# Sums of a Strassen-form down projection moved into gate-and-up, and its seven products taken one after the other over all pairs

## The chip, the core and the metric

The kernel runs on one core of one Trainium2 chip. The metric is the device time of one execution in microseconds (us); each figure is the median of several runs. The engines are TensorE (PE, with its weight loads as PEld), VectorE (DVE), ScalarE (ACT), GpSimd (POOL) and SyncE (SP), which here issues nearly all the DMAs.

## What is computed

One block on x of 1024 tokens x 1024 features in float32. The change touches the two FFNs; between them lies a mixer (an input projection, two kinds of mixing along the tokens, an output projection), which stays as it is.

```python
def swiglu(x, w_gate, w_up, w_down):
    return (jax.nn.silu(x @ w_gate) * (x @ w_up)) @ w_down

x = x + 0.5 * swiglu(rmsnorm(x, ffn1_norm), ffn1_w_gate, ffn1_w_up, ffn1_w_down)
h = rmsnorm(x, mix_norm)
...
x = x + concat([y_a, y_b]) @ w_out
x = x + 0.5 * swiglu(rmsnorm(x, ffn2_norm), ffn2_w_gate, ffn2_w_up, ffn2_w_down)
y = rmsnorm(x, final_norm)
```

w_gate and w_up are 1024 x 2816, w_down is 2816 x 1024.

## The kernel before

**Precision.** Every product keeps float32 accuracy by three matmuls (mm3): each operand is split into a high part (an ACT cast, L61) and a low part (a DVE subtraction, L62), and high x high, high x low and low x high are summed in PSUM.

**Seven products.** Large products are cut 2 x 2 and computed with seven products of sums instead of eight products of blocks. The sums have to be formed beside TensorE.

**Gate-and-up** (`ffn`, loop over c). The 2816 FFN columns are 22 chunks of 128. For each chunk, SP loads two half MB of weights (graw, L186), GpSimd forms four sums (L192), ACT and DVE split them, and PE runs 84 matmuls. Even chunks use four PSUM banks called mm, odd chunks four called ax. DVE and ACT finish the activations sg = silu(gate) * up, which go to DRAM as hd (L280). Chunk 0 is done plainly, by `gu_plain`. The tiles of x that the FFN adds to are loaded after chunk 2 (FFN2 keeps four of the eight in SBUF).

**Down stage.** It multiplies hd (2816 x 1024 tokens) with w_down. Two chunks make a pair, so there are 11 pairs. Pairs 0 to 9 are taken in three groups, of 1 + 1, 2 + 2 and 2 + 2 pairs, and the seven products combine the two pair sets of a group. `group` loads four tiles hx of activations and weights (L300, L301), forms the sums in place on GpSimd (L323; DVE takes some in the first group), splits each product's operands into a tile called unit (three buffers; a unit is two chunks of 128 here), and runs 24 matmuls for each unit. A product's result in its four banks is then added by DVE into the x tiles (L347) or an accumulator acc (L351), or copied by ACT into acc (L354). The plan of a group takes the banks in the order mm, mm, ax, mm, mm, ax, ax: where `start` is true, a new result begins in the banks, which the product before must have left. Units are prepared two ahead of the matmuls. Pair 10 is done plainly at the end, tile of tokens by tile of tokens; after each tile, `emit` hands the finished x tile on: in FFN1 it is stored to xd and normed, and transposed for the mixer (`to_mid`, L520, L95); in FFN2 it is normed and stored to the output (`fin`).

A stage is 936 matmuls of 128 x 128 by 512. The program is written in order and the instructions of each engine are queued in an order that a scheduler makes from it; a queue runs strictly in its order. Of the tiles' pools, gsp has 7 buffers, post 4, cmb 3 and the pool of x tiles 8.

## Time and profile before

| what | value |
|---|---|
| median of 3 runs | 1911.67 us (1911.02 to 1916.76) |
| the profiled execution | 1916.1 us, of which the span is 1914.0 us |
| mean granted TensorE clock | 0.981 |
| GpSimd busy | 665.9 us, 35% |
| DMA traffic | 199.98 MB, mean 104 GB/s |

The page that the profile gives holds the busy time of each engine over the span, slices of it, DMA queues, the chain of work that ended last, and the costliest groups of instructions. Tables by windows and timelines come from the same trace. In a timeline a row reads: start in us, length, engine, line of the kernel, operation, output<-input by the program's names, shape, count, and in brackets the engine's idle time before it and what released it. An engine's share is a mean over stages with different limits, so a stage is read by its own window.

### The profile page before, as it was taken

What the parts mean: (1) busy time and instruction counts of PE and PEld (TensorE: products, weight loads), DVE (VectorE), ACT (ScalarE), POOL (GpSimd) and SP (SyncE); (2) the same over time, 40 slices, a digit from 0 to 9 for tenths busy, and PEclk for the clock granted to TensorE, in tenths of its full rate; (3) what the DMA queues carried; (4) which work ended last, traced back from release to release, by engine and by line L of the source; (5) the groups of instructions that cost most, each with busy time, mean ns of one, the idle gap of its engine ahead of it and who ended that gap; (6) DMA issues with size and microseconds to landing.
All of it is one profiled execution on the core that took longest, in us unless ns stands there. A gap on an engine that the chain in (4) does not pass through costs nothing.

```text
span 1914.0 us, 25049 instructions
## 1 busy us (share of the span) xinstructions
PE 1812.0 (95%) x9759; PEld 1542.0 (81%) x9759; DVE 1253.3 (65%) x1663; ACT 674.2 (35%) x1171; POOL 665.9 (35%) x477
## 2 busy tenths in 40 slices
PE   6999999999798899898999999999999999979888
PEld 5888888887687689797788989988888888768766
DVE  7655555557988984668755236655555555798896
ACT  6333232334233343432354434433333332323233
POOL 4322222224647802221132402242323222454681
PEclk9999999999899999999999999999999999999999
DMA  6222222225222224354432343323232323531312
GB/s 227 92 91 78 88 78 89 77 89 200 89 79 97 84 107 141 122 182 122 130 90 65 118 145 122 115 74 97 68 99 67 99 67 98 171 115 57 119 44 88
DMA packets 95815, 199.98 MB, mean 104 GB/s; under 512 B 23857, under 2 KB 39505, under 8 KB 95697
## 3 DMA queue, kind: packets, MB, share of 16 engines
q1 hardware_dynamic: 93200, 193.95, 30.7%
q10 hardware_dynamic: 2496, 4.44, 0.8%
q8 instruction: 76, 1.25, 0.3%
q14 instruction: 43, 0.34, 0.1%
HBM read 149.06 MB, written 49.30 MB: 104 GB/s over the span
## 4 chain that ended last, share of the span: by engine, by line
PE 71%; DVE 15%; POOL 4%; issue 4%; ACT 3%; DMA 2%; DVEq 0%; POOLq 0%; SPq 0%; ACTq 0%
PE mm L53 40%; PE ax L53 29%; DVE unit L62 6%; DVE x L347 1%; POOL hx L323 1%; DVE acc L852 1%; POOL s L192 1%; PE sd L53 1%; DMA graw<-in_f1gu_dram 1%; PE ax L95 1%; PE sc L53 1%; POOL rs L70 0%; POOL E L778 0%; DVE xn L82 0%; ACT actT L102 0%
## 5 line engine op out<-in xcount | busy, mean ns | idle before, releaser
L53 PE MATMUL mm<-unit 128*128 128x512 f32 x960 | 240.9, 412 | 49.7 <-DVE acc L351 25.8
L62 DVE TENSOR_TENSOR unit<-hx,unit 128x1024 fp32r<-128x1024 f32 x128 | 247.2, 1971 | 45.0 <-ACT unit L61 44.3
L192 POOL TENSOR_TENSOR s<-graw 128x512 f32<-128x512 f32 x84 | 108.5, 1292 | 466.7 <-DMA graw<-in_f1gu_dram 178.9
L53 PEld LDWEIGHTS mm<-unit 128*128 128x128 f32 x960 | 192.0, 201 | 96.6 <-issue 48.9
L62 DVE TENSOR_TENSOR gs<-s,gs 128x512 fp32r<-128x512 f32 x168 | 162.0, 966 | 142.5 <-ACT gs L61 141.7
L61 ACT CAST unit<-hx 128x1024 fp32r<-128x1024 f32 x128 | 128.5, 1050 | 260.9 <-PE mm L53 84.7
L53 PE MATMUL ax<-unit 128*128 128x512 f32 x912 | 211.0, 390 | 4.0 <-DVE unit L62 3.4
L61 ACT CAST gs<-s 128x512 fp32r<-128x512 f32 x168 | 100.2, 620 | 317.9 <-POOL s L192 213.7
L53 PEld LDWEIGHTS ax<-unit 128*128 128x128 f32 x912 | 170.6, 188 | 40.6 <-DVE unit L62 4.2
L53 PE MATMUL ax<-T,gs 128*128 128x512 f32 x792 | 183.1, 389 | 0.0
L53 PEld LDWEIGHTS ax<-T,gs 128*128 128x128 f32 x792 | 148.7, 188 | 30.8
L62 DVE TENSOR_TENSOR ga<-graw,ga 128x512 fp32r<-128x512 f32 x134 | 96.2, 719 | 114.0 <-ACT ga L61 113.7
L53 PE MATMUL mm<-B,ga 128*128 128x512 f32 (+1 forms) x864 | 166.3, 347 | 0.2 <-ACT B L118 0.2
L53 PE MATMUL mm<-T,gs 128*128 128x512 f32 x720 | 166.4, 389 | 0.0
L53 PEld LDWEIGHTS mm<-T,gs 128*128 128x128 f32 x720 | 135.2, 188 | 28.0
L53 PEld LDWEIGHTS mm<-B,ga 128*128 128x128 f32 x864 | 139.7, 194 | 19.5 <-ACT B L118 0.5
L53 PE MATMUL mm<-actT,wk 128*128 128x512 f32 x576 | 152.3, 407 | 1.8 <-ACT ev L713 1.8
L53 PE MATMUL mm<-wk,actT 128*128 128x256 f32 (+1 forms) x1152 | 147.9, 286 | 0.0
L53 PEld LDWEIGHTS mm<-wk,actT 128*128 128x128 f32 x1152 | 141.2, 191 | 0.4
L53 PE MATMUL ax<-B,ga 128*128 128x512 f32 x528 | 126.9, 389 | 0.0
L323 POOL TENSOR_TENSOR hx<-hx 128x1024 f32<-128x1024 f32 x40 | 126.8, 3201 | 0.0
L53 PEld LDWEIGHTS mm<-actT,wk 128*128 128x128 f32 x576 | 105.0, 191 | 21.4 <-ACT ev L713 2.0
(240 smaller groups left out, 2756.4 us busy)
## 6 DMA issues: line engine op xcount, KB each, us to landing
graw<-in_f1gu_dram SPq DMA_DIRECT2D x44, 512.0 KB, 4.3
graw<-in_f2gu_dram SPq DMA_DIRECT2D x44, 512.0 KB, 3.9
hd<-sg SPq DMA_DIRECT2D x42, 512.0 KB, 5.1
hx<-hd SPq DMA_DIRECT2D x40, 512.0 KB, 6.3
hx<-in_f1wd_dram SPq DMA_DIRECT2D x20, 512.0 KB, 6.8
hx<-in_f2wd_dram SPq DMA_DIRECT2D x20, 512.0 KB, 7.4
x<-in_x_dram SPq DMA_DIRECT2D x16, 512.0 KB, 6.1
graw<-in_wo_dram SPq DMA_DIRECT2D x16, 512.0 KB, 3.8
```

The costliest lines, as they stand in the source:

```text
L53: nc.tensor.matmul(*args, **kw)
L61: nc.scalar.copy(h, src)
L62: nc.vector.tensor_tensor(l, src, h, op=ALU.subtract)
L95: nc.tensor.transpose(ps[:, i * P:(i + 1) * P], blk(i), ident)
L192: nc.gpsimd.tensor_tensor(f, u, v, op=op)
L323: eng.tensor_tensor(o, u, v, op=op)
L347: nc.vector.scalar_tensor_tensor(xv, p, 0.5, xv, op0=ALU.mult, op1=ALU.add)
L852: nc.vector.scalar_tensor_tensor(acc, pad[:, j:j + 512], cw[:, blk, j:j + 1], acc, op0=ALU.mult, op1=ALU.add)
```

## The change

The seven products are now formed inside each pair: chunk 2q is one half of the inner dimension and chunk 2q + 1 the other. The sums that this takes are formed in gate-and-up. After an odd chunk's weights are prepared, `weight_sums` loads the pair's rows of w_down (wd), forms four sums on GpSimd and stores them to DRAM as wq; after the odd chunk's products, `hidden_sums` forms four sums of activations on GpSimd and stores seven operands as hq, in place of hd. These tiles live in the pool of x tiles, so the x tiles are loaded after gate-and-up (`load_xts`); FFN2 stores its four kept tiles to xd and loads all eight again.

The down stage runs each of the seven products over all 11 pairs before it goes to the next, in six units of two pairs (the last of one): 7 x 11 x 12 = 924 matmuls. Each unit loads its two operands (left from hq, right from wq or w_down) and splits them. The banks alternate. There is no plain pair at the end: x tiles 0 to 3 are finished after the sixth product, and 4 to 7 in the last units of the seventh.

```diff
--- before.py
+++ after.py
@@ -170,11 +170,18 @@
         for _ in islice(zip_longest(*parts), n):
             pass
-    def ffn(cb, wgu, wd, ps, gp, qp, bp, start, emit, before={}):
+    def ffn(cb, wgu, wd, ps, gp, qp, bp, start, load_xts, emit, before={}):
         A, X = (ps[0], "mm"), (ps[1], "ax")
         gu_s = {}
         B = cb.B
-        hd = [dr.tile([2, P, T], F32, tag=f"hd{i}", name=f"hd{i}") for i in range(NCH // 2)]
+        hq = [dr.tile([P, 7, 2, 512], F32, tag=f"hq{i}", name=f"hq{i}") for i in range(6)]
+        wq = [dr.tile([P, 4, 2, 512], F32, tag=f"wq{i}", name=f"wq{i}") for i in range(6)]
+        hid = {}
+        def whole(name):
+            return xp.tile([P, 2, 512], F32, tag="x", name=name)
         def gtile(dt, name):
             return gp.tile([P, 2, 512], dt, tag="gsp", name=name, bufs=7)
@@ -237,28 +244,25 @@
                 first = x[1] == "1"
                 for p, wt in ((gates[i], g["B11" if first else "a12"]), (ups[i], g["a21" if first else "a22"])):
                     products(p, wt, xs[x], sl, first, not first)
-            sg = gp.tile([P, 2, w], F32, tag="sf", name="sg", bufs=3)
+            if 0 not in hid:
+                hid[0] = whole("sg")
+            sg = hid[0][:, :, sl]
             for i in range(2):
                 nc.scalar.activation(sg[:, i], gates[i], AF.Silu)
                 nc.vector.tensor_tensor(sg[:, i], sg[:, i], ups[i], op=ALU.mult)
-            nc.sync.dma_start(hd[0][0].rearrange("p (b n) -> p b n", b=2)[:, :, sl], sg)
-        def gu(c, pp, sl=slice(0, 512)):
+        def post(n):
+            return qp.tile([P, 2, 512], F32, tag="post", name=n, bufs=4)
+        def gu(c, pp):
             g = gu_s[c]
-            w = sl.stop - sl.start
-            pa, pb, pc, pd = (bank(*pp)[:, :w] for _ in range(4))
+            pa, pb, pc, pd = (bank(*pp) for _ in range(4))
             def prod(p, n, first, last):
-                products(p, g[n], lambda s, k, sl: B[n][:, s, k, sl], sl, first, last)
-            def post(n):
-                return qp.tile([P, 2, 512], F32, tag="post", name=n, bufs=4)
-            if w == 512:
-                pe, up, sg = post("pe"), post("up"), post("sg")
-            else:
-                both, sg = post("pe"), post("sg")
-                pe, up, sg = both[:, :, :w], both[:, :, w:], sg[:, :, :w]
+                products(p, g[n], lambda s, k, sl: B[n][:, s, k, sl], slice(0, 512), first, last)
+            pe, up = post("pe"), post("up")
+            sg = hid[c] = whole("sg")
             p1, e = pe[:, 0], pe[:, 1]
             prod(pa, "B11", True, False)
             nc.scalar.copy(p1, pa)
@@ -277,177 +281,158 @@
             prod(pd, "T4", False, True)
             nc.vector.tensor_tensor(up[:, 0], pd, p1, op=ALU.add)
             nc.vector.tensor_tensor(sg[:, 0], sg[:, 0], up[:, 0], op=ALU.mult)
-            nc.sync.dma_start(hd[c // 2][c % 2].rearrange("p (b n) -> p b n", b=2)[:, :, sl], sg)
+        def sub(o, u, v, op=ALU.subtract):
+            nc.gpsimd.tensor_tensor(o, u, v, op=op)
+        def weight_sums(q):
+            raw = []
+            for j in range(2):
+                raw.append(whole("wd"))
+                nc.sync.dma_start(raw[j], wd[2 * q + j].rearrange("p (s n) -> p s n", s=2))
+            (b11, b12), (b21, b22) = ((r[:, 0], r[:, 1]) for r in raw)
+            t12, t34 = whole("t12"), whole("t34")
+            sub(t12[:, 0], b12, b11)
+            sub(t12[:, 1], b22, t12[:, 0])
+            sub(t34[:, 0], b22, b12)
+            sub(t34[:, 1], b21, t12[:, 1])
+            for i, t in enumerate((t12, t34)):
+                nc.sync.dma_start(wq[q // 2][:, 2 * i:2 * i + 2, q % 2], t)
+        def hidden_sums(q):
+            a, b = hid.pop(2 * q), hid.pop(2 * q + 1)
+            s12, s34 = whole("s12"), whole("s34")
+            h = hq[q // 2][:, :, q % 2]
+            nc.sync.dma_start(h[:, 0], a[:, 0])
+            nc.sync.dma_start(h[:, 1:3], b)
+            sub(s12[:, 0], a[:, 1], b[:, 1], ALU.add)
+            sub(s12[:, 1], s12[:, 0], a[:, 0])
+            sub(s34[:, 0], a[:, 0], a[:, 1])
+            sub(s34[:, 1], b[:, 0], s12[:, 1])
+            for i, t in enumerate((s12, s34)):
+                nc.sync.dma_start(h[:, 3 + 2 * i:5 + 2 * i], t)
         start(SimpleNamespace(load_gu=load_gu, gu=gu, gu_plain=gu_plain, gtile=gtile, A=A, X=X))
         xts = {}
         for c in range(1, NCH):
             together(load_gu(c))
+            if c % 2:
+                weight_sums(c // 2)
             gu(c, (A, X)[c % 2])
+            if c % 2:
+                hidden_sums(c // 2)
             for f in before.get(c, ()):
                 f(xts)
         acc = [gtile(F32, "acc") for _ in range(2)]
+        load_xts(xts)
         def accu(t):
             return acc[t // 2][:, t % 2]
...
+        def to_x(t, f):
+            def ev(i, p):
+                xv = xts[t + i][:, f * 512:f * 512 + 512]
+                nc.vector.scalar_tensor_tensor(xv, p, 0.5, xv, op0=ALU.mult, op1=ALU.add)
+            return ev
+        def new_acc(i, p):
+            nc.scalar.copy(accu(i), p)
+        def end_acc(i, p):
+            nc.vector.tensor_tensor(accu(i), p, accu(i), op=ALU.add)
+            nc.scalar.mul(accu(i), accu(i), 0.5)
+        def fold(t, f):
+            for i in range(4):
+                xv = xts[t + i][:, f * 512:f * 512 + 512]
+                nc.gpsimd.tensor_tensor(xv, xv, accu(i), op=ALU.add)
+        pending = []
+        def emitting(t, ev):
+            def f(i, p):
+                ev(i, p)
+                g = emit(t + i, xts[t + i])
+                if g is not None:
+                    pending.append(g)
+            return f
+        plan = (
+            (0, (0, 0), A, True, False, new_acc, None),
+            (4, 1, X, True, True, end_acc, None),
+            (1, (1, 0), A, False, True, to_x(0, 0), partial(fold, 4, 1)),
+            (3, 0, X, True, False, to_x(4, 1), partial(fold, 0, 1)),
+            (5, 2, A, True, False, to_x(4, 1), partial(fold, 4, 0)),
+            (6, (1, 1), X, False, True, emitting(0, to_x(0, 1)), None),
+            (2, 3, A, False, True, emitting(4, to_x(4, 0)), None),
+        )
+        def prepare(l, r, u):
+            n = 2 if u < 5 else 1
+            left, right = gtile(F32, "left"), post("right")
+            nc.sync.dma_start(left[:, :n], hq[u][:, l, :n])
+            if isinstance(r, tuple):
+                w = wd[4 * u + r[0]:min(4 * u + r[0] + 3, NCH):2][:, :, r[1] * 512:r[1] * 512 + 512]
+                nc.sync.dma_start(right[:, :n], w.rearrange("j p n -> p j n"))
             else:
...
+                nc.sync.dma_start(right[:, :n], wq[u][:, r, :n])
+            t = bp.tile([P, 2, 2, 2, 512], F32R, tag="cmb", name="unit", bufs=3)
+            for i, s in enumerate((left, right)):
+                split(t[:, 0, i, :n], t[:, 1, i, :n], s[:, :n])
+            return t, n
+        def mms(p, t, un, first, last):
+            u, n = un
+            tsl = slice(t * P, t * P + P)
+            for j in range(n):
+                mm3(p, u[:, 0, 0, j, tsl], u[:, 1, 0, j, tsl], u[:, 0, 1, j], u[:, 1, 1, j],
+                    first and j == 0, last and j == n - 1, skip_group_check=True)
+        units = [(k, u) for k in range(7) for u in range(6)]
+        ahead = []
+        def get():
+            while units and len(ahead) < 3:
+                k, u = units.pop(0)
+                ahead.append(prepare(plan[k][0], plan[k][1], u))
+            return ahead.pop(0)
+        banks = {}
+        for k, (_, _, pp, first, last, ev, then) in enumerate(plan):
+            if first:
+                banks[pp] = [bank(*pp) for _ in range(4)]
+            ps = banks[pp]
+            n = 3 if k == 6 else 6
+            for u in range(n):
+                un = get()
                 for t in range(4):
...
+                    mms(ps[t], t, un, first and u == 0, last and u == 5)
+                    if u == 5:
+                        ev(t, ps[t])
+                if pending:
+                    pending.pop(0)()
+            if then is not None:
+                then()
+        for f in pending:
+            f()
+        pending.clear()
+        rest = [get() for _ in range(3)]
+        for t in range(4):
+            for u, un in enumerate(rest):
+                mms(ps[t], t, un, False, u == 2)
+            ev(t, ps[t])
+            if t > 1 and pending:
+                pending.pop(0)()
+        for f in pending:
+            f()
     def psums(stack, n):
         return [pool(stack, f"ps{i}", k, PSUM) for i, k in enumerate(n)]
@@ -514,18 +499,19 @@
         def after(xts):
             st["gm"] = grow("mix_norm")
+        def load_xts(xts):
             xts.update(load_x(xdram, range(8)))
         def to_mid(t, xt):
             nc.sync.dma_start(xd[t], xt)
             if t == 0:
                 st["hT"] = acts()
-                st["xn"] = bp.tile([P, 4, D], F32, tag="cmb", name="xn", bufs=3)
-            xn = st["xn"][:, t % 4]
+            xn = gp.tile([P, D], F32, tag="gsp", name="xn", bufs=7)
             normed(xt, st["gm"], xn)
             return lambda: to_T((ps[1], "ax"), lambda c: xn[:, c * P:(c + 1) * P], t % 4, st["hT"][t // 4])
-        ffn(cb, a["f1gu"], a["f1wd"], ps, gp, qp, bp, start1, to_mid, {2: [after]})
+        ffn(cb, a["f1gu"], a["f1wd"], ps, gp, qp, bp, start1, load_xts, to_mid, {2: [after]})
         hT = st["hT"]
     g2 = grow("ffn2_norm")
@@ -597,6 +583,8 @@
                 normed(x, g2, x, junk)
             together(cb.blocks(i, pp, xi, uv, b, late=True))
         together(second)
+        for t in order[1]:
+            nc.sync.dma_start(xd[t], xs[t])
         def start2(f):
             together(f.load_gu(0, True))
@@ -618,9 +606,10 @@
         st = {}
         def after(xts):
-            xts.update({t: xs[t] for t in order[1]})
-            xts.update(load_x(xd, order[0]))
             st["gf"] = grow("final_norm")
+        def load_xts(xts):
+            xts.update(load_x(xd, range(8)))
         def fin(t, xt):
             o = gp.tile([P, D], F32, tag="gsp", name="o", bufs=7)
@@ -641,7 +630,7 @@
                 nc.vector.scalar_tensor_tensor(o[:, f], xt[:, f], rs, st["gf"][:, f], op0=ALU.mult, op1=ALU.mult)
                 eng.dma_start(odram[t][:, f], o[:, f])
-        ffn(cb, a["f2gu"], a["f2wd"], ps, gp, qp, bp, start2, fin, {2: [after]})
+        ffn(cb, a["f2gu"], a["f2wd"], ps, gp, qp, bp, start2, load_xts, fin, {2: [after]})
```

What stood in `group` and `pair` goes, in the places marked "...". How it moves instructions shows in the orders of the queues. First PE, in FFN1's down stage from its first matmul, of before; mm and ax are the banks:

```order
L53 MATMUL mm<-unit 128x512 x48
L53 MATMUL ax<-unit 128x512 x24
L53 MATMUL mm<-unit 128x512 x48
L53 MATMUL ax<-unit 128x512 x48
L53 MATMUL mm<-unit 128x512 x96
L53 MATMUL ax<-unit 128x512 x48
L53 MATMUL mm<-unit 128x512 x96
L53 MATMUL ax<-unit 128x512 x96
L53 MATMUL mm<-unit 128x512 x96
L53 MATMUL ax<-unit 128x512 x48
L53 MATMUL mm<-unit 128x512 x96
L53 MATMUL ax<-unit 128x512 x132
```

And of the change, from the same place; ident and xn belong to the transposes of finished tiles:

```order
L53 MATMUL mm<-unit 128x512 x132
L53 MATMUL ax<-unit 128x512 x132
L53 MATMUL mm<-unit 128x512 x132
L53 MATMUL ax<-unit 128x512 x132
L53 MATMUL mm<-unit 128x512 x132
L53 MATMUL ax<-unit 128x512 x132
L53 MATMUL mm<-unit 128x512 x14
L95 MATMUL ax<-ident,xn 128x128 x8
L53 MATMUL mm<-unit 128x512 x10
L95 MATMUL ax<-ident,xn 128x128 x8
```

Before, a row of mm mostly holds two products, one behind the other in the same banks; now each row of 132 is one product over all pairs, and the banks change with it.

Second SP, at the end of FFN1's gate-and-up and the entry of its down stage, of before (hd_109 is the last pair's activations):

```order
L280 DMA hd_108<-sg 128x1024
L280 DMA hd_109<-sg 128x1024
L300 DMA hx<-hd_99 128x2x512
L301 DMA hx<-in_f1wd_dram 128x2x512
L300 DMA hx<-hd_100 128x2x512
L301 DMA hx<-in_f1wd_dram 128x2x512
```

And of the change (hq_99 to hq_104 are the operands of the six units, s_ are sums of the last pair, x the tiles that the FFN adds to):

```order
L380 DMA left<-hq_99 128x1024
L383 DMA right<-in_f1wd_dram 128x2x512
L448 DMA x<-in_x_dram 128x1024
L309 DMA hq_104<-sg 128x2x512
L315 DMA hq_104<-s_3623 128x2x512
L315 DMA hq_104<-s_3624 128x2x512
L448 DMA x<-in_x_dram 128x1024 x7
L383 DMA right<-in_f1wd_dram 128x2x512 x2
L383 DMA right<-in_f1wd_dram 128x512
L385 DMA right<-wq_105 128x1024
```

The first right row here is that of the third unit; those of the fourth and fifth (x2) stand behind the stores of the last pair's sums and behind the loads of x.

Third SP again, at the end of FFN1, of before (wz, wv and wqkv are weights of the mixer's input projection, xd is x between the stages):

```order
L409 DMA hx<-hd_109 128x2x1024
L410 DMA hx<-in_f1wd_dram 128x2x1024
L685 DMA raw<-in_wz_dram 128x1088 x2
L685 DMA raw<-in_wv_dram 128x1024 x2
L685 DMA raw<-in_wqkv_dram 128x1024
L685 DMA raw<-in_wz_dram 128x1024
L520 DMA xd<-x 128x1024 x8
```

And of the change:

```order
L507 DMA xd<-x 128x1024 x3
L380 DMA left<-hq_101 128x1024
L380 DMA left<-hq_102 128x1024
L380 DMA left<-hq_103 128x1024
L380 DMA left<-hq_104 128x512
L507 DMA xd<-x 128x1024 x4
L674 DMA raw<-in_wz_dram 128x1088 x2
L674 DMA raw<-in_wv_dram 128x1024 x2
```

The mixer's first weights were issued ahead of the eight stores to xd and now stand behind them; the last product's operands stand behind the stores of the first four tiles.

More of the change, by code (lines that the diff above doesn't have):

```diff
@@ L292, in ffn @@
         acc = [gtile(F32, "acc") for _ in range(2)]
+        load_xts(xts)
         def accu(t):
             return acc[t // 2][:, t % 2]
-        def load_x(x, pairs, th, dh):
-            for i, q in enumerate(pairs):
-                ks = slice(2 * i, 2 * i + 2)
-                nc.sync.dma_start(x[:, 0, ks], hd[q][:, :, th * 512:th * 512 + 512].rearrange("j p n -> p j n"))
-                nc.sync.dma_start(x[:, 1, ks], wd[2 * q:2 * q + 2][:, :, dh * 512:dh * 512 + 512].rearrange("j p n -> p j n"))
@@ L407, in pair @@
-        def pair(q):
-            raw = ap.tile([P, 2, 2, T], F32, tag="actT", name="hx")
-            nc.sync.dma_start(raw[:, 0], hd[q].rearrange("j p n -> p j n"))
-            nc.sync.dma_start(raw[:, 1], wd[2 * q:2 * q + 2].rearrange("j p n -> p j n"))
-            def prep(i):
-                t = bp.tile([P, 2, 2, T], F32R, tag="cmb", name="unit", bufs=3)
-                for j in range(2):
-                    split(t[:, 0, j], t[:, 1, j], raw[:, i, j])
-                return t
-            return prep
@@ L448, in ffn @@
-        for f in done[8:]:
-            if f is not None:
-                f()
+        def to_x(t, f):
[8 more added lines that the diff above has]
+            nc.scalar.mul(accu(i), accu(i), 0.5)
```

115 lines of the change are left out of this document (removed).

## The prediction

> **What bounds the kernel now.** I read the totals of each engine first, then the chain that ended last, then a table by stage, then what TensorE waits for.
>
> ```profile
> PE 1812.0 (95%) x9759; PEld 1542.0 (81%) x9759; DVE 1253.3 (65%) x1663; ACT 674.2 (35%) x1171; POOL 665.9 (35%) x477
> ...
> PE 71%; DVE 15%; POOL 4%; issue 4%; ACT 3%; DMA 2%; DVEq 0%; POOLq 0%; SPq 0%; ACTq 0%
> ```
>
> PE is busy 95% of the span and holds 71% of the chain; the 15% of DVE has to lie in stages where PE waits. A table of four stretches shows where: gate-and-up of FFN1, its down stage, then the same two of FFN2. The first 7 us of the program stand under it, as a sample of nearly pure loading.
>
> ```profile
> core 0: us, PE busy (x) PEld busy (x) DVE busy (x) ACT busy (x) POOL busy (x), PEclk, DMA share, GB/s
> 95.40:457.10 361.70, 361.70 (x1597) 299.62 (x1596) 198.87 (x264) 112.00 (x188) 94.57 (x73) 1.00 0.29 92
> 457.10:714.30 257.20, 229.81 (x985) 186.71 (x984) 230.81 (x198) 92.99 (x108) 141.18 (x57) 0.94 0.29 101
> 1295.50:1657.20 361.70, 361.70 (x1597) 299.63 (x1596) 198.84 (x265) 111.88 (x188) 93.77 (x73) 1.00 0.29 91
> 1657.20:1906.20 249.00, 222.69 (x937) 181.02 (x936) 218.13 (x181) 82.15 (x92) 141.35 (x56) 0.95 0.25 88
> ```
>
> ```profile
> 457.10:500.00 42.90, 37.07 (x148) 29.41 (x147) 39.59 (x38) 15.87 (x19) 18.84 (x8) 0.92 0.59 204
> ...
> 0.70:8.00 7.30, 0.00 (x0) 0.00 (x0) 0.22 (x2) 2.95 (x4) 0.56 (x1) 1.00 0.82 287
> ```
>
> Gate-and-up is pure PE: 361.70 of 361.70 us, at a granted clock of 1.00. The down stages are not: PE idles 257.2 - 229.8 = 27.4 us in FFN1 and 249.0 - 222.7 = 26.3 us in FFN2, and the clock falls to 0.94 and 0.95. DVE is busy 90% of FFN1's down stage. The change touches all four stretches, so its price falls in the full ones and its gain in the two with holes. What PE waits for, then FFN2's down stage on PE (start, length, what ran, in brackets the idle time before it):
>
> ```profile
> PE mm L53 <- DVE acc L351: 25.8, 4, 7.1
> PE mm L53 <- DVE x L347: 19.9, 4, 6.8
> ```
>
> ```profile
> 1677.29 5.60 PE L53 MATMUL mm<-unit 128*128 128x512 f32 x24
> 1686.07 7.32 PE L53 MATMUL mm<-unit 128*128 128x512 f32 x24 [3.17 <-DVE x L347]
> ...
> 1722.29 13.48 PE L53 MATMUL mm<-unit 128*128 128x512 f32 x48 [7.14 <-DVE acc L351]
> 1735.61 11.04 PE L53 MATMUL ax<-unit 128*128 128x512 f32 x48
> 1746.49 13.76 PE L53 MATMUL mm<-unit 128*128 128x512 f32 x60
> ```
>
> Eight waits, 45.7 of the 53.7 idle us, have one form: a product in the mm banks follows another in the mm banks, and cannot start until DVE has emptied them (L347, L351). DVE does that late, since it stands in order behind splits that GpSimd's sums slow down:
>
> ```profile
> L323 POOL TENSOR_TENSOR hx<-hx 128x1024 f32<-128x1024 f32 x40 | 126.8, 3201 | 0.0
> ...
> L61 ACT CAST unit<-hx x128: 1031/1052/1060, 446.5 to 1880.0; 128x1024 fp32r<-128x1024 f32 x128
> L62 DVE TENSOR_TENSOR unit<-hx,unit x128: 1204/1226/3432, 447.6 to 1882.5; 128x1024 fp32r<-128x1024 f32 x128
> ```
>
> A split's subtraction takes 1.23 us at the median and up to 3.43.
>
> **Part 1, the down stage.** The pitch of undisturbed matmuls is (1746.49 - 1735.61) / 48 = 0.2267 us. Before, FFN2's stage is 936 of them, 212.2 us, plus 26.3 idle, plus slow matmuls after a wait: the 48 behind the wait of 7.14 took 13.48 where the next 48 took 11.04, so 2.4; the four long waits cost some 8.8 together, and 1.7 is left over. After, there are 7 products of 11 pairs, 7 x 11 x 12 = 924 matmuls, 209.5 us. Products alternate between mm and ax, so a bank has the whole length of another product, about 30 us, to be emptied: I cost the eight waits at nothing. L323's forty sums leave the stage, so a unit of two pairs needs DVE for 2 x 1.23 = 2.45 us and ACT for 2 x 1.05 = 2.1, beside PE's 24 x 0.2267 = 5.44. Three unit buffers cover that. If the cover went, the waits would be back (a rival below). The sums into x that GpSimd keeps, 12 per stage, lie behind whole products.
>
> ```profile
> 154.70 0.33 SPq L280 DMA_DIRECT2D hd<-sg  x1
> ```
>
> ```profile
> graw<-in_f1gu_dram SPq DMA_DIRECT2D x44, 512.0 KB, 4.3
> ...
> hd<-sg SPq DMA_DIRECT2D x42, 512.0 KB, 5.1
> ```
>
> What is late next is the data. Each unit loads both operands, 1.05 MB in 5.44 us, 193 GB/s. The two sampled rows put full use near 204 / 0.59 = 346 and 287 / 0.82 = 350 GB/s (estimates), so 55% of it: enough once the pipe is full. At the entry it isn't: the load of the fourth unit's weights stands on SP behind three stores of the last hidden sums and eight loads of x, which before came early in gate-and-up. The stores wait for GpSimd. From the last chunk's start (19.04 us long, next part) the stores can go from about 22 us; 5.8 MB (three stores, seven loads of x, the fourth unit's weights, half a MB each) at 346 GB/s are 16.7 us, to 38.7; about 3 for issuing eleven transfers at 0.33 (the SP row above), and 1.05 + 1.23 for the split, make 44.0. Three units are over at 19.0 + 3 x 5.44 = 35.4. **Entry wait 8.6 us, and 2.4 for slow matmuls behind it: 11 us per FFN.** Bounds: 4 (loads overlap better than one behind the other) and 20 (the last loads of x also wait for two stores to land, about 5 us each as hd's).
>
> The Trainium skill ("HBM Reference", Specifications) says that a core streaming alone measures about 425 GB/s. By it the 5.8 MB would take 13.6 us and the sum would fall by some 6 us over both FFNs; the two rows here give 350 at most, and I stay with them.
>
> In the last product the loads of its third to sixth unit stand behind the stores of four finished tiles, xd or out: I add 2 us in FFN1 and 1 in FFN2 (0 to 5). FFN1's stage also holds five tiles' transposes, now as before:
>
> ```profile
> 694.05 1.03 PE L95 MATMUL ax<-ident,xn 128*128 128x128 f32 x8
> 694.84 2.99 PE L53 MATMUL ax<-unit 128*128 128x512 f32 x12
> ...
> 710.99 3.35 PE L53 MATMUL ax<-unit 128*128 128x512 f32 x12
> ...
> 717.12 2.54 PE L53 MATMUL mm<-wk,actT 128*128 128x264 f32 x19
> ...
> 721.06 25.14 PE L53 MATMUL mm<-wk,actT 128*128 128x264 f32 x206
> ```
>
> Eight transposes take 0.79 us up to the next matmul, about 0.95 with what they slow: 4.8 for five. FFN1: 209.5 + 11 + 2 + 4.8 + 1 = 228.3, **29 less than 257.2**. FFN2: 209.5 + 11 + 1 = 221.5, **27.5 less than 249.0**.
>
> **Part 2, FFN1 to the mixer.** The last unit's matmuls end at 714.34. The mixer's stream, wk, starts in effect at 717.0 (206 in 25.14 are 0.122 each; 34 of them ran ahead of 721.06): 2.7 later. Its first weights were loaded long before; now these loads stand on SP behind the last tile's store to xd.
>
> ```profile
> raw<-in_wz_dram SPq DMA_DIRECT2D x2, 544.0 KB, 8.3
> ```
>
> About 1.5 for the last tile's sum and the store's issue, 8.3 for landing, 1.05 + 1.23 for a split like a unit's: 12.1 against 2.7, **9.4 more**. With a landing of 4.3, as for graw, it is 5; with one landing more for the second half, 14.
>
> **Part 3, gate-and-up.** A pair of chunks takes 38.1 us. GpSimd gets eight sums of the kind of L192 in these rows, 8 x 1.29 = 10.3 us, on top of 10.3. Traffic grows from 3.1 MB a pair (four graw, two hd) to 6.0 (weights read, their sums and seven hidden parts stored): 83 to 158 GB/s, under half of 346. PE has no hole, so all of it must fit beside PE:
>
> ```profile
> 152.48 2.88 PE L53 MATMUL mm<-B,ga 128*128 128x512 f32 x12
> ...
> 158.62 1.29 POOL L192 TENSOR_TENSOR s<-graw 128x512 f32<-128x512 f32 x1 [11.71 <-DMA graw<-in_f1gu_dram]
> ...
> 161.96 1.12 DVE L62 TENSOR_TENSOR gs<-s,gs 128x512 fp32r<-128x512 f32 x1 [3.15 <-ACT gs L61]
> ...
> 163.60 0.68 DVE L62 TENSOR_TENSOR gs<-s,gs 128x512 fp32r<-128x512 f32 x1
> ...
> 164.81 1.47 DVE L62 TENSOR_TENSOR gs<-s,gs 128x512 fp32r<-128x512 f32 x1
> ...
> 171.52 2.88 PE L53 MATMUL ax<-B,ga 128*128 128x512 f32 x12
> ...
> 174.24 1.07 PE L53 MATMUL ax<-T,gs 128*128 128x512 f32 x4
> ```
>
> The chunk is 171.52 - 152.48 = 19.04 us. The tightest product is T2 of the next chunk: split by 163.1 and used at 174.24, 11 us of slack. On SP the second half of graw now queues behind stores that wait for GpSimd, some 3 us later, and it lands later, some 2 more: about 6 us of slack stay. **I cost it at nothing**; past the slack each us would be paid at up to 20 chunk pairs, some 20 us. Below nothing is excluded by the busy share.
>
> GpSimd costs DVE time where both run: the subtraction at 164.81, beside a sum, took 1.47 us, the one at 163.60 took 0.68. The Trainium skill ("SBUF — State Buffer", Who interferes with whom) makes this a lock: a DVE instruction with two SBUF inputs and a GpSimd instruction reading SBUF block each other for the whole instruction. By it eight sums could hold DVE for 10.3 us more in 38.1, from 55% busy to 82%; the two rows agree in kind.
>
> **Part 4, small.** FFN2's first norms on GpSimd now stand behind three sums of chunk 1, 3.9 us, mostly hidden: +1 (0 to 6). The start and the last 7.8 us are as before: 0.
>
> **Sum**, against the profiled execution of 1916.1 us (span 1914.0): -29 - 27.5 + 9.4 + 1 = -46.1, so 1870. That execution lies 4.4 above the median of 1911.67, so I predict **1866**.
>
> **Rivals.** The first is the same mechanism with a better entry: fourth weights and wz land in time, both entries cost 4 and the handoff 5: 1866 - 14 - 4.4 - 3 = 1845. (3 being the late loads of the last product.) For it: loads share 16 engines and need not queue one behind the other. Against: SP issues in order, and the stores wait for sums.
>
> The second: banks aren't the reason, and PE still waits at a product's end, for units or for DVE. Then about 45 us stay and the change does nothing: 1911. For it: DVE is at 90%. Against: that load is L323's neighbour, and L323 leaves.
>
> The third: gate-and-up loses its cover. If each pair's T2 or T4 comes 1 to 2 us late, 20 pairs cost 20 to 40: 1886 to 1906. For it: 1.47 against 0.68, and SP's stores that wait for GpSimd ahead of graw. Against: 11 us of slack.
>
> The fourth is slower than before: the down stage is bound by transfers. A stage holds 38.5 units' worth; the gain of 46 is gone when each stage takes 23 us more, (209.5 + 23) / 38.5 = 6.04 us a unit, that is when DMA sustains less than 1.05 MB / 6.04 = 174 GB/s. At 150 a unit takes 7.0 us and the time is near 1940. For it: the whole program averages 88 to 101 GB/s in these stages. Against: 204 at a share of 0.59 in the entry window, with the same kind of loads.
>
> **How the numbers follow.** Forecast, 1850 to 1886: 0.66. Better entry, 1838 to 1850: 0.10. Gate-and-up loses, 1886 to 1906: 0.11. No effect: 0.06. Transfer-bound: 0.07. The range takes the forecast with the bounds of entry and handoff, most of the better entry and over half of the third rival: 1843 to 1898. A measurement of this kernel can tell 0.3%, 5.7 us, from no change: faster 0.87, within it 0.06, slower 0.07.
>
> **What would show it.** Right: gate-and-up windows of 361.7 with PE full; no wait for L347's or L351's successors; one wait of some 8 us after the third unit; wk starting 12 us after the last unit; down windows of 228 and 222. Wrong: waits inside gate-and-up on DVE gs, waits on unit spread over the down stage, or a clock that stays at 0.95 there.

## The result, and the profile after

The changed kernel takes 1988.0 us (median of 4 runs, 1983.5 to 1992.0) against 1913.2 (median of 4, 1911.0 to 1916.8): a ratio of 1.039 with an interval of 1.036 to 1.042, slower. I had forecast 1866, with a range of 1843 to 1898: the measured time lies above it, and the change loses where a gain was forecast.

The totals of each engine and the chain that ended last, of the changed kernel's page:

```profile
PE 1838.3 (92%) x9735; PEld 1555.0 (78%) x9735; DVE 1158.1 (58%) x1535; ACT 676.1 (34%) x1191; POOL 715.5 (36%) x577
...
PE 37%; issue 21%; POOL 20%; DVE 12%; DMA 5%; ACT 4%; SPq 1%; POOLq 0%; DVEq 0%; ACTq 0%
PE mm L53 21%; PE ax L53 13%; POOL s L286 6%; POOL t L286 6%; POOL s L199 6%; DVE gs L62 2%; ACT gs L61 1%; DVE ga L62 1%; DVE up L274 1%; DMA right<-in_f1wd_dram 1%; DVE sg L280 1%; DMA left<-hq 1%; DMA right<-in_f2wd_dram 1%; DVE acc L841 1%; PE sd L53 1%
```

PE fell from 71% of the chain to 37%, and GpSimd rose from 4% to 20%, on the lines of the new sums (L286) and of the sums of gate and up weights (L199, L192 before). The table by stretch, in the same four pieces as before: chunks 3 to 21 of FFN1's gate-and-up, its down stage, and the same two of FFN2.

```profile
core 0: us, PE busy (x) PEld busy (x) DVE busy (x) ACT busy (x) POOL busy (x), PEclk, DMA share, GB/s
101.80:513.90 412.10, 378.70 (x1597) 307.40 (x1595) 245.05 (x264) 108.41 (x187) 216.37 (x147) 0.96 0.43 143
513.90:740.60 226.70, 216.74 (x965) 178.50 (x965) 127.06 (x131) 93.43 (x116) 33.97 (x24) 0.98 0.60 207
1344.00:1755.20 411.20, 381.61 (x1597) 309.22 (x1596) 246.03 (x266) 109.61 (x189) 217.54 (x148) 0.96 0.43 144
1755.20:1978.20 223.00, 213.55 (x925) 174.91 (x924) 121.29 (x119) 86.64 (x104) 33.35 (x22) 0.98 0.60 206
```

Gate-and-up, full before, is 50 us longer in each FFN, with 33 and 30 us in which PE idles; the same 1597 matmuls also keep it busy 17 and 20 us longer, at a granted clock of 0.96. The down stages are 30.5 and 26.0 us shorter. Taken over the whole span (profiled executions, stretches cut at the same matmuls):

| stretch | before | after | difference |
|---|---|---|---|
| start to FFN1's chunk 1 | 55.2 | 56.3 | +1.1 |
| FFN1, chunks 1 to 21 | 401.9 | 457.6 | +55.7 |
| FFN1, down stage | 257.2 | 226.7 | -30.5 |
| last unit of FFN1 to FFN2's first plain half chunk | 509.2 | 522.3 | +13.1 |
| FFN2, plain chunk | 29.8 | 36.8 | +7.0 |
| FFN2, chunks 1 to 21 | 403.9 | 455.5 | +51.6 |
| FFN2, down stage | 249.0 | 223.0 | -26.0 |
| tail | 7.8 | 9.7 | +1.9 |
| span | 1914.0 | 1987.9 | +73.9 |

What PE waits for, three groups of the changed kernel (in each: us in total, number of waits, longest):

```profile
PE mm L53 <- DVE up L274: 59.6, 20, 4.3
PE mm L53 <- ACT unit L61: 17.3, 3, 8.9
...
PE ax L53 <- DVE up L274: 9.9, 8, 1.9
```

The eight waits for L347 and L351 are gone. In their place stand 20 waits of 3.0 us in the even chunks of gate-and-up, for L274 (L270 before), a DVE sum that reads the bank of the product T3 (a chunk's seven products are, in order, B11, T2, T1, T3, B21, B22 and T4); eight shorter ones for it stand in odd chunks. The row with ACT unit holds the two waits for a fourth unit that were forecast:

```profile
540.78 15.92 PE L53 MATMUL mm<-unit 128*128 128x512 f32 x60 [8.87 <-ACT unit L61]
```

```profile
1780.88 17.03 PE L53 MATMUL mm<-unit 128*128 128x512 f32 x60 [8.14 <-ACT unit L61]
```

One even chunk of the timeline shows how the 20 waits arise. First the rows of before that set the scale, in the chunk that starts at 152.48:

```profile
154.10 0.33 SPq L186 DMA_DIRECT2D graw<-in_f1gu_dram  x1
...
164.21 0.68 DVE L270 TENSOR_TENSOR up<-mm,pe 128x512 f32<-128x512 f32 x1
...
168.80 2.88 PE L53 MATMUL mm<-T,ga 128*128 128x512 f32 x12
```

and the same places of the changed kernel, in the chunk that starts at 295.31:

```profile
295.31 2.88 PE L53 MATMUL mm<-B,ga 128*128 128x512 f32 x12
...
298.03 8.32 PE L53 MATMUL mm<-T,gs 128*128 128x512 f32 x36
...
302.87 0.36 SPq L315 DMA_DIRECT2D hq<-s  x1
303.34 1.00 SPq L193 DMA_DIRECT2D graw<-in_f1gu_dram  x1
...
310.03 1.28 POOL L199 TENSOR_TENSOR s<-graw 128x512 f32<-128x512 f32 x1 [7.18 <-DMA graw<-in_f1gu_dram]
...
313.34 1.09 DVE L62 TENSOR_TENSOR gs<-s,gs 128x512 fp32r<-128x512 f32 x1 [8.99 <-ACT gs L61]
314.36 0.68 DVE L274 TENSOR_TENSOR up<-mm,pe 128x512 f32<-128x512 f32 x1
...
315.09 4.60 PE L53 MATMUL mm<-T,ga 128*128 128x512 f32 x12 [3.30 <-DVE up L274]
```

The load of the second half of the next chunk's weights is issued 8.0 us into the chunk, right behind the last store of sums, where it was issued at 1.6. The sum that needs it starts 6.7 us after the issue instead of 4.5. The split waits for that sum, and DVE idles 9 us for the split. L274 stands behind that split: its own product T3, the last of the 36 matmuls from 298.03, is done by 306.2, and it starts at 314.36. PE needs the bank for T4. The 12 matmuls behind the wait then take 4.60 instead of 2.88 us.

### The profile page after: what moved, and what is told of

It is laid out like the page before. It is cut to its first block, busy times and chain, and to the rows that moved or that the text cites. A ratio compares the mean times of both kernels' runs of the same rounds, so it can differ in the third digit from the quotient of the medians.

```text
span 1987.9 us, 25450 instructions
## 1 busy us (share of the span) xinstructions
PE 1838.3 (92%) x9735; PEld 1555.0 (78%) x9735; DVE 1158.1 (58%) x1535; ACT 676.1 (34%) x1191; POOL 715.5 (36%) x577
## 4 chain that ended last, share of the span: by engine, by line
PE 37%; issue 21%; POOL 20%; DVE 12%; DMA 5%; ACT 4%; SPq 1%; POOLq 0%; DVEq 0%; ACTq 0%
PE mm L53 21%; PE ax L53 13%; POOL s L286 6%; POOL t L286 6%; POOL s L199 6%; DVE gs L62 2%; ACT gs L61 1%; DVE ga L62 1%; DVE up L274 1%; DMA right<-in_f1wd_dram 1%; DVE sg L280 1%; DMA left<-hq 1%; DMA right<-in_f2wd_dram 1%; DVE acc L841 1%; PE sd L53 1%
## 5 line engine op out<-in xcount | busy, mean ns | idle before, releaser
L62 DVE TENSOR_TENSOR gs<-s,gs 128x512 fp32r<-128x512 f32 x168 | 154.1, 936 | 274.1 <-ACT gs L61 274.0
L53 PE MATMUL mm<-unit 128*128 128x512 f32 x1056 | 248.7, 396 | 19.4 <-ACT unit L61 17.3
L53 PEld LDWEIGHTS mm<-unit 128*128 128x128 f32 x1056 | 200.3, 191 | 64.7 <-ACT unit L61 18.8
L199 POOL TENSOR_TENSOR s<-graw 128x512 f32<-128x512 f32 x84 | 108.9, 1296 | 271.3 <-DMA graw<-in_f1gu_dram 135.8
L62 DVE TENSOR_TENSOR unit<-left,unit 128x1024 fp32r<-128x1024 f32 x84 | 102.6, 1222 | 144.0 <-ACT unit L61 143.7
L53 PE MATMUL ax<-unit 128*128 128x512 f32 x792 | 180.5, 389 | 0.0
L53 PEld LDWEIGHTS ax<-unit 128*128 128x128 f32 x792 | 148.7, 188 | 30.8
L62 DVE TENSOR_TENSOR ga<-graw,ga 128x512 fp32r<-128x512 f32 x134 | 157.5, 1176 | 13.8 <-ACT ga L61 13.5
L61 ACT CAST unit<-left 128x1024 fp32r<-128x1024 f32 x84 | 82.5, 982 | 242.9 <-PE ax L53 107.0
L53 PEld LDWEIGHTS mm<-B,ga 128*128 128x128 f32 x864 | 139.8, 194 | 19.1 <-DVE B L119 0.4
L53 PE MATMUL mm<-T,ga 128*128 128x512 f32 x240 | 86.7, 530 | 59.6 <-DVE up L274 59.6
L70 POOL TENSOR_TENSOR rs<-rs,half 128x1 f32<-128x1 f32 (+1 forms) x29 | 20.2, 697 | 331.8 <-DVE rs L76 330.4
```

The lines of the kernel that those rows point to most:

```text
L53: nc.tensor.matmul(*args, **kw)
L61: nc.scalar.copy(h, src)
L62: nc.vector.tensor_tensor(l, src, h, op=ALU.subtract)
L70: nc.gpsimd.tensor_tensor(o, i, half[:, :w], op=ALU.pow)
L199: nc.gpsimd.tensor_tensor(f, u, v, op=op)
```

## The experiments

Theory 1: SP holds the weights' load behind stores that wait for GpSimd, and on DVE the late split holds L274. The rival: GpSimd's added work as such, by the port that it shares with DVE.

**The order on DVE alone.** T2's and T1's subtractions stand behind L274:

```diff
+        def behind_ev():
+            return tc.issue_after(last_ev[0]) if last_ev else nullcontext()
...
-            g["T2"] = sp("s2", s2)
+            with behind_ev():
+                g["T2"] = sp("s2", s2)
...
+            last_ev[:] = [nc.vector.tensor_tensor(up[:, 1], pd, e, op=ALU.add).ins]
```

(and the same for T1)

> Only the order on DVE is changed: the subtractions of the next chunk's T2 and T1 splits stand behind the sum that empties the T3 bank (up, L274 of the changed kernel), not ahead of it. Theory 1 (in each even chunk PE's T4 waits for L274, which stands on DVE behind a split whose GpSimd sum is late): the 20 waits of 3.3 us and the slow matmuls behind them go, gate-and-up falls from 457.6 to about 403 us in FFN1 and from 455.5 to about 405 in FFN2, the time from 1988 to 1880-1895. Rival (the late sum itself is what PE lacks, or GpSimd holds DVE up): the wait moves to the next chunk's T2, some 3 us per pair, and the time stays at 1950-1990.

Measured: 1965.1 us (1964.1 and 1966.2), still slower than before. On PE and GpSimd, one even chunk and the start of the next:

```profile
283.22 2.88 PE L53 MATMUL mm<-B,ga 128*128 128x512 f32 x12
...
299.90 2.88 PE L53 MATMUL mm<-T,ga 128*128 128x512 f32 x12
302.62 2.88 PE L53 MATMUL ax<-B,ga 128*128 128x512 f32 x12
...
304.03 1.29 POOL L203 TENSOR_TENSOR s<-graw 128x512 f32<-128x512 f32 x1 [7.29 <-DMA graw<-in_f1gu_dram]
...
307.36 0.73 PE L53 MATMUL ax<-T,gs 128*128 128x512 f32 x2 [1.86 <-ACT gs L61]
```

T4 no longer waits, so L274's place on DVE did make the wait where it was. But T2 of the next chunk now waits: its sum starts 20.8 us after the even chunk's start at 283.22, where it started 14.7 us after it in the changed kernel. The loop closes on itself: later splits give later activations, later hidden sums, later stores, and the load behind these stores later still. In this chunk the first hidden sum starts 7.2 us after the chunk's start where it started 1.2 us after it, and the load is issued at 14.0 us instead of 8.0. Theory 1's first half holds, its number fell, and the rival on record came out: the wait moves to the next T2, and the late load is a loss by itself.

**The order on SP alone.** The four stores of a pair's hq are queued behind the weights of the chunk two later:

```diff
+            if c % 2 and late:
+                with tc.issue_after(last_graw[0]):
+                    late.pop()()
...
             gu(c, (A, X)[c % 2])
             if c % 2:
-                hidden_sums(c // 2)
+                late.append(hidden_sums(c // 2))
```

(hidden_sums forms the sums as before and returns its four stores as a function; last_graw is the last load of weights)

> Only the order on SP is changed: the four stores of hq of a pair stand behind the second half of the weights (graw) of the chunk two later, not ahead of it. Theory 1 (the weights are late because SP holds their load behind stores that wait for GpSimd's sums, and behind these stores' data): that load goes some 5 us sooner and lands sooner, its sum starts 6 to 7 us sooner, the waits for L274 fall from 3.3 us to under 0.5, the time to 1880-1900. Rival (GpSimd's eight added sums hold DVE up through the shared port, or are too much work for GpSimd): sums, traffic and bytes are the same, so the waits stay at 2.5 us or more, the time at 1960-1990.

Measured: 1890.0 us (2 runs, 1885.1 and 1894.9), 0.987 of before (0.979 to 0.995). The same windows of gate-and-up:

```profile
95.90:457.60 361.70, 361.70 (x1597) 299.52 (x1596) 236.95 (x264) 111.33 (x188) 206.86 (x146) 1.00 0.48 165
1289.80:1651.60 361.80, 361.80 (x1598) 299.55 (x1596) 242.01 (x264) 112.14 (x188) 207.80 (x146) 1.00 0.48 165
```

PE is full again, to a tenth of a microsecond of before, with the same added sums (GpSimd 207 us, 95 before) and more traffic in less time. Work of GpSimd, bytes and the shared port are therefore not what cost 100 us; one queue's order is.

**Half the GpSimd sums left out**, in the changed kernel:

> The four GpSimd sums of activations of each pair are left out (the unsummed tiles are stored in their place, with the same bytes); the four sums of down weights stay. Theory 1: the stores of hq now wait for DVE's last product sg alone, 2.9 us sooner, so the load behind them goes at about 5.1 us into the chunk instead of 8.0, still behind the stores' data; the waits for L274 fall from 3.3 us to 0.3-1.2, the time to 1890-1925. Rival (the work of GpSimd as such, by the shared port): half of the added sums gone, half of the loss gone, 1930-1945, with DVE's own durations, not the start of the weights' load, as what changes.

Measured: 1884.5 us in one run. This doesn't tell as much as it was meant to. With the sums gone, the scheduler also put the stores of hq behind the weights' loads (in one chunk the loads at 305.40, the stores from 309.59), so that both things changed at once; it only agrees with the run above.

**The entry of the down stage.** On top of stores_late, the x tiles' loads are queued behind the weights of the second product's first units:

```diff
-        load_xts(xts)
...
                 un = get()
+                if (k, u) == (1, 3):
+                    with tc.issue_after(last_right[0]):
+                        load_xts(xts)
```

> On the kernel stores_late, the eight loads of x are issued on SP behind the last weights of the second product's first units, not ahead of the fourth unit's weights. Theory 1 (PE's one wait in each down stage is for the fourth unit's weights, which queue behind x): the wait of 8.4 to 8.9 us after the third unit falls under 2 us and the slow matmuls behind it go, the down stages get 9 to 11 us shorter each, the span goes from 1883 to 1861-1867. Rival (the units' buffers come free late, or transfers as such are slow there): a wait of 5 us or more stays at the third or fourth unit, the span above 1873.

Measured: 1860.8 us in one run. The two down stages:

```profile
457.40:672.60 215.20, 214.43 (x965) 177.61 (x965) 126.65 (x131) 92.81 (x115) 34.94 (x24) 1.00 0.61 213
1638.30:1849.30 211.00, 210.12 (x925) 173.11 (x923) 120.31 (x119) 86.24 (x104) 33.38 (x22) 1.00 0.62 214
```

The wait is gone, the clock is 1.00, and FFN2's stage takes 211.0 us, 1.5 above the 209.5 of 924 undisturbed matmuls.

**Is it the banks?** On stores_late, the second and third product of the plan are exchanged, so that products follow each other in the same banks twice:

```diff
             (0, (0, 0), A, True, False, new_acc, None),
-            (4, 1, X, True, True, end_acc, None),
-            (1, (1, 0), A, False, True, to_x(0, 0), partial(fold, 4, 1)),
+            (1, (1, 0), A, False, True, to_x(0, 0), None),
+            (4, 1, X, True, True, end_acc, partial(fold, 4, 1)),
             (3, 0, X, True, False, to_x(4, 1), partial(fold, 0, 1)),
```

> On the kernel stores_late, two products are exchanged, so that the banks go mm, mm, ax, ax, mm, ax, mm: two pairs of products follow each other in the same banks, in each FFN. Nothing else moves, and GpSimd forms no sums there. Theory 1 as I predicted it (alternating banks remove the waits, 5.7 us each before, with 2.2 of slow matmuls behind): four waits come back, of 2 to 7 us, and the span grows by 14 to 34 us to 1897-1917. Rival (the waits were long because DVE stood behind splits slowed by GpSimd's sums, which are gone whatever the banks do): the waits are the bare emptying of a bank, under 1.5 us, and the span grows by under 12 us.

Measured: 1884.5 us in one run, against 1885.1 and 1894.9. On PE, FFN1's first four products:

```profile
483.17 45.98 PE L53 MATMUL mm<-unit 128*128 128x512 f32 x192 [8.34 <-ACT unit L61]
528.99 60.12 PE L53 MATMUL ax<-unit 128*128 128x512 f32 x264
```

Two products in ax run as 264 matmuls without a gap, and the mm row crosses its border too. The rival holds: with GpSimd's sums out of the stage, alternating the banks was worth nothing here. Whether it would have helped with the sums kept, no run shows. So the same was tried from the other side, **the kernel before without the sums of its down stage** (L323's on GpSimd and those of DVE in the first group), its order of banks kept:

> The kernel before, with all the sums of its down stage (L323, on GpSimd and in the first group on DVE) left out; units are split from the unsummed tiles. Loads, splits, matmuls and the order of the banks stay. Theory (the waits at the products' ends came from DVE standing behind splits that take 3.3 us beside GpSimd's sums; the order of the banks matters little): splits take 1.2 us, the waits for L347 and L351 fall from 45.7 us to under 10, the span from 1914 to 1858-1872. Rival (the same banks one after the other are what costs, as I predicted): waits of 30 us or more stay, the span above 1890.

Measured: 1844.1 us in one run. Its two down stages:

```profile
457.90:679.50 221.60, 218.71 (x983) 180.38 (x982) 163.75 (x194) 91.47 (x106) 24.38 (x19) 1.00 0.34 117
1621.00:1834.50 213.50, 212.63 (x937) 175.59 (x935) 154.89 (x178) 80.87 (x91) 25.26 (x18) 1.00 0.30 103
```

257.2 and 249.0 us fall by 35.6 and 35.5, nearly all that the waits and slow matmuls cost: 2.9 and 0.9 us of idle PE are left. In FFN1's stage DVE's 194 instructions take 163.8 us, where 198 took 230.8 before. What happened in the kernel before stands in its own timeline, ahead of the longest wait:

```profile
1708.24 13.30 DVE L62 TENSOR_TENSOR unit<-hx,unit 128x1024 fp32r<-128x1024 f32 x4
...
1721.47 2.47 DVE L351 TENSOR_TENSOR acc<-mm,acc 128x512 f32<-128x512 f32 x4
```

Four subtractions of a kind that takes 1.22 us at the median of before_no_sums took 3.3 each beside GpSimd's sums, and L351, which PE needed, stood behind them. The run takes away more than this neighbourhood: the splits' waits for the sums, and DVE's own sums, go with it. That the slow subtractions are the larger part is read from DVE's busy time and this timeline.

**FFN2's start.** First, on stores_late, GpSimd's sums of chunk 1 behind the norms' powers:

```diff
+            if c == 1:
+                with tc.issue_after(last_pow[0]):
+                    together(load_gu(c))
```

> On the kernel stores_late, GpSimd's sums of chunk 1 are queued behind the norms' powers (rs) at both FFNs' start. Theory 1 (FFN2's entry lost 7 us because rs stands behind three sums that wait for their weights): from the end of the first plain chunk to chunk 1, 25.4 us in stores_late, falls to 19-21; the span falls by 4 to 6 us to 1877-1879. Rival (it is lost to DVE or to the four stores and loads of x): it stays within 1.5 us.

Measured: 1883.1 us in one run; the plain chunk takes 37.8 us (1207.66 to 1245.41), 37.1 in stores_late. (The expectation counted 25.4 from the first half's end.) It failed. Then, on x_late, the four late norms ahead of the first plain half chunk in the program:

```diff
-            f.gu_plain(slice(0, 256), b)
             xns = {}
...
                     normed(xs[i + 4 * j], g2, xns[i][j])
+            f.gu_plain(slice(0, 256), b)
```

> On the kernel x_late, FFN2's four late norms stand ahead of the first plain half chunk in the program, so that ScalarE squares their tiles before it waits for that half's banks to apply silu. Theory (the 7 us at FFN2's entry are these squares standing behind silu on ScalarE): from the first plain half to chunk 1 it falls from 37 us to 30-32, the span from 1859 to 1852-1855. Rival (the tiles or their memory are late): it stays within 1.5 us.

Measured: one run of 1848.0 us, and in the timed run below a median of 1857.2. The plain chunk falls from 36.9 to 34.0 us (1191.42 to 1225.45). On ScalarE, x_late first and then norm_first:

```profile
1206.97 0.38 ACT L252 ACTIVATE sg<-mm 128x256 f32<-128x256 f32 x1 [4.11 <-PE mm L53]
1207.25 1.05 ACT L74 ACTIVATE xn<-x 128x1024 f32<-128x1024 f32 x1
```

```profile
1183.44 1.06 ACT L74 ACTIVATE xn<-x 128x1024 f32<-128x1024 f32 x1 [2.72 <-DVE x L575]
```

The square had stood behind a silu that waits for PE and now runs as soon as its tile is done. This is 2.9 of the 7 us; what makes the rest wasn't found.

**The handoff to the mixer.** First, on stores_late, the first two weight loads from ScalarE's queue:

> On the kernel stores_late, the first two weight loads of the mixer are issued from ScalarE's queue, not from SP. Theory 1 (they are late because they queue on SP behind the eight stores of x): the mixer's first matmul with weights, 11.3 us behind the last unit's end in stores_late, comes 3 to 6 us sooner, the span falls by 3 to 6 us to 1877-1880. Rival (their memory is still in use by the last units' tiles until the down stage ends): the start moves by less than 1.5 us.

Measured: 1885.6 us in one run. Nothing gained: ScalarE issued them at 692.68, behind its own work, 5.4 us later than SP had (687.29). That told nothing of the memory. Then, on x_late, other buffers for xn and the loads ahead of the last stores of x:

```diff
-            xn = gp.tile([P, D], F32, tag="gsp", name="xn", bufs=7)
+            xn = qp.tile([P, D], F32, tag="post", name="xn", bufs=4)
...
+        if n_load[0] < 2:
+            for t in range(4, 8):
+                tc.add_manual_dep(xd_stores[t], ins.name, mybir.DependencyInfo(mybir.DependencyClass.NoSync, mybir.DependencyReason.DATA), reason="order")
```

> On the kernel x_late, xn uses the buffers of the right operands instead of those of the left, and the mixer's first two weight loads are issued ahead of the last four stores of x. Theory (the second load waits for the memory of the last tile's xn, until its transposes have run, and the first stands behind the stores): the mixer's first matmul with weights comes 5 us or less behind the last unit's end instead of 11.3, the span falls from 1859 to 1848-1853. Rival (the transposes and the split's own chain set the start): it stays within 2 us.

Measured: 1867.6 us in one run. On SP, and on PE:

```profile
652.03 1.98 SPq L691 DMA_DIRECT2D raw<-in_wz_dram  x2
```

```profile
668.67 3.66 PE L53 MATMUL mm<-unit 128*128 128x512 f32 x15
...
684.60 1.03 PE L53 MATMUL mm<-wk,actT 128*128 128x264 f32 x3 [3.89 <-ACT wk L61]
```

The weights were loaded 20 us ahead of the last unit's end, and the first matmul still came 12.4 us behind it (11.4 in x_late). My theory fell: neither the queue nor the memory alone sets this start. PE waits for ScalarE's cast, which ran at 683.45, behind the last tile's copies and ScalarE's own issues of loads. That order on ScalarE is the cause is read from the timeline alone; no run changed it.

**All orders mended**, and all but wz_early, timed:

> The changed kernel with every order mended: stores_late, x_late, norm_first and wz_early together. If the losses add up as the single runs show (gate-and-up 105 us, entries 24, handoff 7 to 10, FFN2's start 5 to 7), the time is 1840-1850, 0.963-0.968 of before; if the last two don't hold, 1855-1861.

> The kernel norm_first again, timed: the changed kernel with three orders mended (stores of hq behind the weights, x loaded late, FFN2's late norms ahead of the plain half chunk). Theory: the one look of 1848.0 holds, 1845-1851, 0.964-0.968 of before, 2 to 6 us under the kernel all (1852.4), since wz_early's order cost 6 us by itself. Rival: it lies with all, at 1852 or above, and what wz_early cost is spread between runs.

Measured: all 1852.4 us (median of 6, 1849.6 to 1861.5), 0.968 of before (0.964 to 0.971); norm_first 1857.2 (median of 6, 1851.5 to 1864.5), 0.972 (0.969 to 0.974). Both beat both kernels. Between them the intervals overlap, and the single run of norm_first had given 1848.0: executions of these kernels differ by some 12 us, so single runs above are read by their windows, and their totals only where much more is at stake.

## Why the prediction was wrong

- **Part 1, the down stages, by size: right.** I forecast 228.3 and 221.5 us; they took 226.7 and 223.0. The wait at the fourth unit was put at 8.6 and came at 8.9 and 8.1, and x_late shows its cause to be the one named, loads of x ahead of the fourth unit's weights. That it came out so closely is partly luck. From the last chunk's start the first of the stores went at 25.8 and 24.0 us where I had put 22, the third unit ended at 37.2 and 36.6 instead of 35.4, and from the first store to the fourth unit's first matmul 20.3 and 20.7 us passed instead of 22.0. By the Trainium skill's 425 GB/s ("HBM Reference", Specifications) these 22.0 would have been 18.9, an estimate. The measured times lie between the two, and the loads of this entry ran at 384 GB/s for 15 us (last section), not at the 346 of my rows. The 2 and 1 us for late loads of the last product hardly came: PE has no wait there in FFN1 and one of 0.5 us in FFN2.
- **Part 1, by reason: half wrong.** I wrote that a bank "has the whole length of another product, about 30 us, to be emptied: I cost the eight waits at nothing". The waits went, but not for that: adjacent puts products behind each other in the same banks and has no wait at these borders, and before_no_sums keeps all of before's order and has three waits there of 0.8 to 1.4 us, 3.1 in all, where 45.7 stood. What went was L323 beside the splits. I had read it as the reason why DVE is late, and then credited the banks with the cure.
- **Part 2, the handoff: right in size for its start** (11.5 us from the last unit to wk's first matmul against 12.1; up to FFN2 13.1 us were lost against 9.4), **wrong in cause.** Loads on SP alone don't set it, as wz_early shows.
- **Part 3, gate-and-up: the step that failed.** "I cost it at nothing"; it cost 55.7 + 51.6 = 107 us. Three errors stand in it. The slack: I measured 11 us from T2's split to T2's matmul. But on DVE the sum that empties T3's bank stands behind that split; it ended at 164.9 and PE needed it at 168.8, so 3.9 us was all. The delay: I took 5 us; it was 6.4 from SP's order and 2.2 from landing, 8.6. Of these, 7.3 reach L274, which starts 11.7 us into the chunk before and 19.1 after, since in the changed kernel one split stands ahead of it instead of two; 7.3 less 3.9 is 3.4, and the wait was 3.3. And the loop: with 3.9 us of slack the wait is paid once in each pair, and what is late feeds the next pair's stores, which dve_order shows when the first waiting place is taken away.
- **The third rival** named stores on SP that wait for GpSimd ahead of graw, and gave it 0.11 and 1 to 2 us a pair. It was the case, at 3.0 us of wait a pair and up to 2.6 of slow matmuls: of FFN1's ten even chunks, the 12 matmuls behind the wait took 4.3 to 5.5 us in eight.
- **The shared port.** The Trainium skill's rule ("SBUF — State Buffer", Who interferes with whom) that such instructions of DVE and GpSimd block each other was weighed in the wrong stage. In gate-and-up it is real and harmless: DVE's busy time grew from 198.9 to 237.0 us in stores_late's window, and PE lost nothing; that is 4.0 us a pair, not the 10.3 that I had held possible by the rule. In the down stage of before, before_no_sums gave back 36 us per FFN, of which the port's own part is not shown apart from the waits for the sums. There the trace agrees with the rule in kind and nearly in number: 1.22 us of DVE and 2.40 us of GpSimd (the shortest of its sums in that timeline), one after the other, would make 3.6 (an estimate by the rule), and side by side they took 3.3 each.
- **Part 4:** FFN2's start was forecast at +1 (0 to 6) and cost 7.0, for another reason than the one named: rs_first did nothing, norm_first gave back 2.9.

## What to carry to other kernels

The slack of a load ends at the first instruction that stands behind its consumer on an in-order queue and that somebody else waits for, not at the consumer's own use. Before work is put into a full stage, follow each queue that it is put on: which instruction stands behind the new wait, who waits for that, and whether the chain comes back to the new work in the next round. And when a wait goes, undo each half of the change alone before one believes which half did it.

## What the runs showed of the hardware that was not expected

I had taken 346 to 350 GB/s as full use of the DMA engines, scaled up from shares of 0.59 and 0.82. The changed kernel moves more, and not only for a moment. The window in which seven loads of x and the weights behind them land, at the entry of FFN1's down stage:

```profile
526.00:541.00 15.00, 6.13 (x28) 4.77 (x27) 2.35 (x4) 2.71 (x3) 0.00 (x0) 0.78 1.03 384
```

384 GB/s stand here over 15 us, at a share of 1.03 as the table counts it. In gate-and-up, over 290 to 342 us in slices of 1.3 us each, such rates come in short stretches:

```profile
GB/s 0 0 0 0 198 202 3 0 0 262 375 383 246 238 309 407 221 0 0 0 0 0 120 284 239 164 8 380 290 255 76 0 0 0 0 0 0 129 271 16
```

Both are nearer to the 425 of the Trainium skill ("HBM Reference", Specifications) than my figure. The down stages of x_late move 213 GB/s at a share of 0.61, which scales to 349: a rate scaled up from such a share understated what full use moved here. Why, the runs don't show.
